# Eleven pairs of heads of the mixer's input projection by Strassen's seven products

## The chip, the cores and the metric

The kernel runs on one core of a Trainium2 chip. The metric is the device time of one execution in microseconds (us). Three timed runs of the kernel before took 2134.25, 2134.5 and 2135.26 us (median 2134.5). The execution whose trace is read here took 2134.78 us; its span, from the first to the last instruction, is 2133.1 us, so 1.7 us lie outside the trace.

## The reference, cut to what matters

A trunk of two layers over 1024 tokens of width 1024, all in float32. Each layer has a token mixer, a norm, a squared-ReLU MLP with a gated embedding beside it, and a norm. The mixer of layer 0 is a pooling, that of layer 1 a gated DeltaNet, whose input projection is the subject here:

```
proj = x @ w_in                                   # 1024x1024 by 1024x4112
qkv, z, b_logit, a_logit = split(proj)            # Q, K, V, z: 8 heads of 128 columns each
qkv = silu(causal_depthwise_conv(qkv, conv_w))    # 4 taps along the tokens
q, k = l2_normalize(q), l2_normalize(k)
beta, g = sigmoid(b_logit), -exp(a_log) * softplus(a_logit + dt_bias)
o = chunk_gated_delta_rule(q, k, v, g, beta)      # 64-token chunks: a triangular solve in each, a scan over them
o = rms_norm(o) * norm_w * silu(z)
mix = o @ w_out
```

The MLP is `square(relu(x @ w1)) @ w2`, with 4096 hidden columns.

## The kernel before, in words

**Products.** Every large product is made in three TensorE matmuls: each operand is cut into a rounded high part and the rest (`split`, L66: a ScalarE copy L68, then a VectorE subtraction L69), and `mm3` (L71, its matmuls L73 to L75) adds high by high, high by rest and rest by high. A full matmul is 128 rows deep, 128 columns of stationary weights wide, and streams 512 columns.

**Order of work.** The stages follow one another: layer 0's mixer, first MLP, DeltaNet, second MLP. `mlp` (L320) already goes by Strassen's scheme. Its first part (L400 ff.) makes the hidden columns in 16 pairs of blocks; a pair is seven products P1 to P7 of twelve matmuls each, 112 products in all, sums of weight blocks are made by VectorE in `prep_a` (L347) three products ahead, and `multiply_a` (L381) runs the products and combines them: P1, P6, P7 and P4 accumulate one after another in one PSUM bank, with a ScalarE copy of the bank between them (L400, L405, L409). Its second part has 56 steps of 24 matmuls, fed by `prep_b` (L451).

**The projection** (`project`, L713) goes over 66 *units*: a unit is one head of K, Q, z or V, or the two gates' columns ("ba"), by half the tokens (512), in 24 matmuls (16 for "ba"), in the order K, Q, z, V (L910 to L914). `load_wsm` (L77) loads a unit's weights and splits them (one 128x1024 split for two units of K, Q and z, for one of V). `conv_a` (L889) convolves a unit of K, Q or V: two ScalarE passes over the PSUM bank and three VectorE passes (L901), then Silu (L902); the results stay in SBUF in six tiles of 16 KB per partition. `z_out` (L904) sends z to DRAM. `at(u, f)` hangs side work on unit u: the decays, the norms of K and Q (`norm2`, transposes on TensorE), `couple` (L822, K by K), then the triangular solve: `lanes_load` fetches a tile L with all 128 blocks, `substitute(m)` eliminates column m in it on VectorE (62 of them, L860 and L862), `lanes_store` and `lanes_turn` send the inverse back to DRAM.

**The scan** (`chain`, L987) goes over 8 chunks of 128 tokens. `load(n)` fetches chunk n's inverse, decays, K transposed and z; `kq`, `kv` and `state_in` read K, Q and V of the chunk from the SBUF tiles through `hc`. `prepare` does chunk 0's part ahead of `run`.

**What sets the order.** The code is straight-line; the framework's list scheduler lays each engine's instructions out once, when the kernel is built, earlier code first among what is ready, and sets the semaphores. On the chip each engine, and SyncE's DMA queue, runs its list in order. Tiles come from pools: `big` has 10 tiles of 16 KB per partition, `wsm` two each of "wh" and "wl", `rawp` three, `tmp` six of 2 KB.

Of the kernel before, what the change touches and what calls it, by code (L numbers as in the profile page):

```python
# [15 lines left out]
P = 128  # L16
S = 1024
# [15 lines left out]
def trunk(ctx: ExitStack, tc: tile.TileContext, io: dict):  # L33
# [286 lines left out]
    def mlp(i, r1, cut_t3, acc, row, finish=None, ahead=None, out=None):  # L320
# [14 lines left out]

        P1, P2, P6, P5, P7, P4, P3 = range(7)
# [3 lines left out]
        with tc.tile_pool(name=f"mlp{i}", bufs=5) as q:  # L340
# [231 lines left out]
    kt_d = dram.tile([8, P, H, P], F32, name="kt_d")  # L572
    ad_d = dram.tile([2, H, 8, 64, 64], F32, name="ad_d")
# [128 lines left out]
    left = mlp(0, r1, cut_t3, acc, 1, finish, ahead)  # L702
# [10 lines left out]
    def project(gd, pool, x2, left, first, heads, g, ex, ahead):  # L713
# [58 lines left out]

        dec = [new_big(F32, "dec").rearrange("p (n c) -> p n c", n=8) for _ in range(2)]
# [90 lines left out]
        def lanes_store():  # L864
# [3 lines left out]
            lanes["Lt"] = new_big(F32, "Lt").rearrange("p (i j) -> p i j", i=64)  # L868

        def lanes_turn(q):  # L870
            L, lt, c = lanes["L"], lanes["Lt"], slice(q * 8, q * 8 + 8)
            A.copy(lt[0:64, c], L[0:64].rearrange("p i j -> p j i")[:, c])
            if q == 7:
                nc.sync.dma_start(t_d.rearrange("h n i j -> (h n) i j"), lt[0:64])
# [9 lines left out]
        def head_tile(s, hf):  # L884
            if (s, hf) not in heads:
                heads[s, hf] = new_big(F32, s).rearrange("p (h c) -> p h c", h=8)
            return heads[s, hf]

        def conv_a(s, h, j, hf, ps):  # L889
            xin = pool.tile([P, 516], F32, tag="xin", name=nm("xin"), bufs=2)  # L890
            y = head_tile(s, hf)[:, h, :]
# [10 lines left out]
            return lambda: A.activation(y, y, AF.Silu)  # L902
# [12 lines left out]
        jof = {"ba": 32, "K": 8, "Q": 0, "z": 24, "V": 16}  # L915
# [14 lines left out]
        K = [head_tile("K", 0), head_tile("K", 1)]  # L930
# [6 lines left out]
        at(20, lanes_load)  # L937

        m, room = 62, 0.0
        for u in range(22, 58):  # L940
            room += 2.2 if u < 34 else 4.2 if u < 50 else 1.5
            while m > 0 and (room > 0 or u == 57):
                at(u, substitute, m)
                room -= 0.4 + 2.1e-3 * m * (63 - m)
                m -= 1
        at(58, lanes_store)
        for q in range(8):
            at(58 + q // 2, lanes_turn, q)
        for k in range(16):
            at(36 + k, lambda k=k: norm2([heads["Q", 0], heads["Q", 1]], g["qn"], k // 2, k % 2))  # L950
        for u, f in ahead:
            at(u, f)
        w = dict(first)

        def weights(k):
            if k < len(units):
                s, h, hf = units[k]
                key = (s, h) if s != "V" else (s, h, hf)
# [5 lines left out]
        for u, (s, h, hf) in enumerate(units):  # L964
# [18 lines left out]
            if fin:  # L983
                fin()
        q_scales()

    def chain(gd, heads, g, ex):  # L987

        hc = lambda s, n, h: heads[s, n // 4][:, h, n % 4 * P:(n % 4 + 1) * P]
# [5 lines left out]
        g4 = lambda gi: slice(gi * 4, gi * 4 + 4)  # L995

        def load(n):
# [12 lines left out]
            nc.sync.dma_start(szt, sz_d[:, :, n * P:(n + 1) * P].rearrange("h d t -> d h t"))  # L1010
# [126 lines left out]
        def prepare():  # L1137
            both(kq, 0)
# [166 lines left out]
```

## Time and profile before

| | busy us | share of the span |
|---|---|---|
| TensorE (PE) | 2106.5 | 99% |
| VectorE (DVE) | 1530.4 | 72% |
| ScalarE (ACT) | 1070.9 | 50% |
| GpSimd (POOL) | 40.3 | 2% |

The profiled execution took 2134.78 us (span 2133.1). The DMA engines moved 308.83 MB at a mean of 145 GB/s; the granted TensorE clock was 0.998 of full speed. "Busy" for TensorE covers overlapping matmuls: one matmul's record is longer than the distance to the next. The shares are means over stages; the first MLP runs from about 172 to 787 us, the projection from 787 to 1190, the scan to about 1302, and the rest of layer 1 to the end.

### The profile page before, as it was taken

To read this page: it belongs to the slowest core of one execution; us is meant where nothing else is said; L and a number is where in the kernel's file an instruction comes from. 1 tells how busy PE (TensorE), PEld (TensorE's weight loads), DVE (VectorE), ACT (ScalarE), POOL (GpSimd) and SP (SyncE) were. 2 spreads that over 40 slices of the span, in tenths; PEclk is the share of its full clock that TensorE was granted. 3 is DMA by queue.
4 is the path that set the end of the run, shared out by engine and by line. 5 is a ranking of instruction groups with operands and counts; after the bars stand their busy time and mean duration, and the time that the engine had idled before them with its cause. 6 is when DMAs were issued, how large, how long until landed. Compare 5 with 4: busy or idle time off the path is not lost.

```text
span 2133.1 us, 27623 instructions
## 1 busy us (share of the span) xinstructions
PE 2106.5 (99%) x10242; PEld 1763.7 (83%) x10242; DVE 1530.4 (72%) x2571; ACT 1070.9 (50%) x1830; POOL 40.3 (2%) x101
## 2 busy tenths in 40 slices
PE   8999999999999999999999999999999999999998
PEld 7888888888888888888888998888888888888887
DVE  7996666668754777879986687499666666875476
ACT  6434555554333457753456676443455555433343
POOL 0000000000000001101001000000000000000000
PEclk9999999999999999999999999999999999999999
DMA  8324444469332333451233655312344445943232
GB/s 307 115 84 148 153 148 144 163 211 335 116 117 99 138 108 104 140 152 50 85 134 114 178 174 178 128 35 86 126 146 163 153 153 185 325 161 119 96 132 88
DMA packets 166154, 308.83 MB, mean 145 GB/s; under 512 B 40258, under 2 KB 62146, under 8 KB 165700
## 3 DMA queue, kind: packets, MB, share of 16 engines
q1 hardware_dynamic: 161412, 298.68, 42.0%
q10 hardware_dynamic: 4608, 8.39, 1.1%
q8 instruction: 80, 1.31, 0.3%
q14 instruction: 54, 0.44, 0.1%
HBM read 212.66 MB, written 94.37 MB: 144 GB/s over the span
## 4 chain that ended last, share of the span: by engine, by line
PE 95%; DVE 2%; ACT 1%; DMA 1%; issue 1%; SPq 0%; DVEq 0%; ACTq 0%
PE ps L73 29%; PE ps L75 29%; PE ps L74 29%; PE ps L143 1%; PE ps L1075 1%; PE ps L1097 1%; PE ps L828 1%; PE ps L799 1%; PE ps L1068 1%; PE ps L1040 1%; PE ps L1063 1%; PE ps L1084 1%; DMA raw<-in_xTt 1%; PE ps L1033 0%; PE ps L1051 0%
## 5 line engine op out<-in xcount | busy, mean ns | idle before, releaser
L74 PE MATMUL ps<-rl,lh 128*128 128x512 f32 x896 | 348.6, 389 | 0.0
L73 PE MATMUL ps<-rh,lh 128*128 128x512 f32 x880 | 342.7, 389 | 0.0
L75 PE MATMUL ps<-rh,ll 128*128 128x512 f32 x880 | 342.3, 389 | 0.0
L68 ACT CAST lh<-raw 128x1024 fp32r<-128x1024 f32 x112 | 118.1, 1055 | 325.5 <-PE ps L74 313.3
L69 DVE TENSOR_TENSOR rl<-w,rh 128x1024 fp32r<-128x1024 f32 x108 | 131.9, 1224 | 178.1 <-issue 107.9
L73 PE MATMUL ps<-xh,wh 128*128 128x512 f32 x512 | 202.7, 396 | 0.0
L75 PE MATMUL ps<-xh,wl 128*128 128x512 f32 x512 | 200.0, 391 | 1.1 <-DVE wl L69 1.1
L73 PE MATMUL ps<-xh,wo 128*128 128x512 f32 x512 | 199.6, 390 | 1.4 <-ACT c L409 1.4
L74 PE MATMUL ps<-xl,wh 128*128 128x512 f32 x512 | 199.4, 390 | 0.0
L75 PE MATMUL ps<-xh,wo 128*128 128x512 f32 x512 | 199.2, 389 | 0.0
L74 PE MATMUL ps<-xl,wo 128*128 128x512 f32 x512 | 199.2, 389 | 0.0
L74 PEld LDWEIGHTS ps<-rl,lh 128*128 128x128 f32 x896 | 168.2, 188 | 34.8
L75 PEld LDWEIGHTS ps<-rh,ll 128*128 128x128 f32 x880 | 165.2, 188 | 34.7 <-DVE ll L69 0.4
L73 PEld LDWEIGHTS ps<-rh,lh 128*128 128x128 f32 x880 | 165.2, 188 | 34.0
L69 DVE TENSOR_TENSOR wo<-raw,wo 128x512 fp32r<-128x512 f32 x192 | 132.1, 688 | 49.9 <-ACT wo L68 49.8
L68 ACT CAST wo<-raw 128x512 fp32r<-128x512 f32 x192 | 119.2, 621 | 96.1 <-PE ps L75 66.1
L339 DVE TENSOR_TENSOR c<-ps,c 128x512 f32<-128x512 f32 x96 | 66.3, 691 | 130.3 <-PE ps L75 67.8
L73 PE MATMUL ps<-xt,wo 128*128 128x512 f32 x384 | 149.6, 390 | 1.5 <-ACT c L400 1.5
L75 PE MATMUL ps<-xt,wo 128*128 128x512 f32 x384 | 149.5, 389 | 0.0
L74 PE MATMUL ps<-xt,wo 128*128 128x512 f32 x384 | 149.4, 389 | 0.0
L69 DVE TENSOR_TENSOR ll<-raw,lh 128x1024 fp32r<-128x1024 f32 x112 | 136.4, 1220 | 1.4 <-ACT lh L68 1.1
L68 ACT CAST rh<-w 128x1024 fp32r<-128x1024 f32 x108 | 112.8, 1047 | 4.4 <-DVE rl L69 2.5
(308 smaller groups left out, 4173.5 us busy)
## 6 DMA issues: line engine op xcount, KB each, us to landing
raw<-h_d SPq DMA_DIRECT2D x112, 512.0 KB, 3.2
raw<-in_w SPq DMA_DIRECT2D x64, 512.0 KB, 3.8
w<-in_w SPq DMA_DIRECT2D x32, 1024.0 KB, 7.6
h_d<-c SPq DMA_DIRECT2D x64, 512.0 KB, 2.8
raw<-in_w_in SPq DMA_DIRECT2D x41, 512.0 KB, 3.5
h_d<-hs SPq DMA_DIRECT2D x32, 512.0 KB, 3.5
pp_d<-tmp ACTq DMA_DIRECT2D x32, 256.0 KB, 3.0
raw<-in_gate SPq DMA_DIRECT2D x16, 512.0 KB, 4.2
```

What stands on the lines that cost most here:

```text
L68: A.copy(hi, src)
L69: V.tensor_tensor(lo, src, hi.bitcast(F32), ALU.subtract)
L73: T.matmul(ps, lh, rh, start=first, stop=False, skip_group_check=more)
L74: T.matmul(ps, lh, rl, start=False, stop=False, skip_group_check=more)
L75: T.matmul(ps, ll, rh, start=False, stop=last, skip_group_check=more)
L143: T.transpose(pss[q][:, j, :], y[:, k * P:(k + 1) * P], ident)
L339: add = lambda o, a, b: V.tensor_tensor(o, a, b, ALU.add)
L799: T.transpose(ps[:, j, :], chunk(tiles, half * 4 + j, h), ident)
L828: T.matmul(ps[:, j, :], kc, kc, start=True, stop=True)
L1040: T.matmul(pq[:, j, :], hc("K", n, h), hc("Q", n, h), start=True, stop=True)
L1063: T.matmul(pk[:, j, :], hc("K", n, h), St[:, h, :], start=True, stop=True)
L1068: T.matmul(pq[:, j, :], hc("Q", n, h), St[:, h, :], start=True, stop=True)
```

## The change

Of the 32 heads of Q, K, V and z, 22 (all of Q and V, six of z) are now projected in 11 pairs. A pair is a 256-column by 1024-token product of depth 1024, made of seven products of 12 matmuls (stationary 128 columns, 512 tokens, depth 512) in place of eight. K, "ba" and two heads of z stay units (22 of them).

The weights' sums, cut into two parts, are made in the first MLP (`pair_parts`: 8 parts for each pair, 88 in all). 60 of them run in the MLP's first part, after products 4 to 107, four to every seven products; 28 in its second part, after steps 8 to 35. They go to DRAM (`ws_d`, 7 tiles of 512 KB a pair) and are fetched again five products ahead of their use. The tokens' sums (`right_a`, `right_b`) are made on the units 9, 11, 18 and 19. `substitute` moves from units 22 to 57 into the pairs (products 3 to 67 of 77), `lanes_store` to product 68, `lanes_turn` to 69 to 72 in eight small tiles, `load0` to 74. K, Q and V go to DRAM (`kqv_d`) and come back by chunk. In a pair the convolution takes all 1024 tokens of a head at once.

```diff
-    def mlp(i, r1, cut_t3, acc, row, finish=None, ahead=None, out=None):
+    def mlp(i, r1, cut_t3, acc, row, finish=None, ahead=None, out=None, side=()):
...
                 multiply_a(*o)
+                if side and 4 <= n < 108 and n * 64 // 112 != (n - 1) * 64 // 112:
+                    side.pop(0)()
...
+                if side and n >= 8:
+                    side.pop(0)()
...
+    pairs = [("Q", 0), ("V", 0), ("z", 2), ("Q", 2), ("V", 2), ("z", 4), ("Q", 4), ("V", 4), ("Q", 6), ("V", 6), ("z", 6)]
...
+    def pair_parts(p):
...
+        def load(key, f, z):
+            t[key] = new_tmp(F32, key)
+            nc.sync.dma_start(t[key], io["w_in"][j + f][:, 4 * z:4 * z + 4, :].rearrange("p k c -> p (k c)"))
+        def cut(k, src=None):
+            hi, lo = new_tmp(F32R, "hi"), t.pop("lo") if src is None else new_tmp(F32R, "lo")
+            src = lo.bitcast(F32) if src is None else src
+            split(hi, lo, src)
+            nc.sync.dma_start(ws_d[p][k][:, 0], hi.bitcast(F32))
+            nc.sync.dma_start(ws_d[p][k][:, 1], lo.bitcast(F32))
+        def s_of(k, o, a):
+            add(t[o], t[o], t[a])
+            cut(k, t[o])
+        return [lambda: (load("a1", 0, 0), load("b1", 1, 0)),
+                lambda: (load("b2", 1, 1), cut(0, t["a1"])),
+                s3,
+                lambda: cut(5, t["b2"]),
+                lambda: (s_of(3, "b1", "b2"), load("a2", 0, 1)),
+                lambda: s_of(2, "a1", "b1"),
+                lambda: cut(1, t["a2"]),
+                lambda: s_of(6, "a2", "a1")]
...
+            def fin():
+                A.activation(y, y, AF.Silu)
+                nc.sync.dma_start(kqv_d[hf * 4:hf * 4 + 4, :, 0, h, :].rearrange("n p c -> p n c"),
+                                  y.rearrange("p (n c) -> p n c", n=4))
...
+            def head(s, h, x, y, n):
+                if s == "z":
+                    A.activation(y, x, AF.Silu)
+                    A.activation(y, y, AF.Copy, scale=nw[:, 0:1])
+                    nc.sync.dma_start(sz_d[h], y)
+                    return
+                A.activation(y, x, AF.Copy, scale=cw[:, j, 3:4])
+                for c in (2, 1, 0):
+                    V.scalar_tensor_tensor(y[:, d:S], x[:, 0:S - d], cw[:, j, c:c + 1], y[:, d:S], ALU.mult, ALU.add)
+                later(n + 1, done, s, h, y, n + 1)
...
+                for kk in range(4):
+                    mm3(ps, o[:, 0, kk, :], o[:, 1, kk, :], right[k][0][:, kk, :], right[k][1][:, kk, :],
+                        new and kk == 0, kk == 3, not new)
+                if k == P1:
+                    A.copy(x11, ps)
+                elif k == P2:
+                    V.tensor_tensor(x11, ps, x11, ALU.add)
+                elif k == P6:
+                    A.copy(x12, ps)
+                elif k == P7:
+                    A.copy(x22, ps)
+                    V.scalar_tensor_tensor(x22, d["ps"][2], -1.0, x22, ALU.mult, ALU.subtract)
+                elif k == P4:
+                    A.activation(x21, ps, AF.Copy, scale=-1.0)
+                    later(n + 1, head, s, h + 1, x[:, 1], x[:, 3], n + 1)
+                elif k == P3:
+                    V.tensor_tensor(x12, ps, x12, ALU.add)
+                    later(n + 1, head, s, h, x[:, 0], x[:, 2], n + 1)
...
-        units += [("Q", h, hf) for h in range(8) for hf in range(2)]
-        units += [("z", h, hf) for h in range(8) for hf in range(2)]
-        units += [("V", h, hf) for hf in range(2) for h in range(8)]
+        units += [("z", h, hf) for h in range(2) for hf in range(2)]
...
+        def right_a(e):
+            mi(r, part(b[1, 1][0], e), part(b[1, 2][0], e))
+            pl(r, r, part(b[1, 1][1], e))
+            mi(r, r, part(b[1, 2][1], e))
+            cut(1, e, r)
+            neg_mi(r2[e], r, b[2, 2], e)
+            cut(2, e, r2[e])
+        def right_b(e):
+            neg_mi(r, r2[e], b[1, 1], e)
+            cut(3, e, r)
+            neg_mi(r2[e], r2[e], b[2, 1], e)
...
+        by_pairs(pool, ts, b)
...
+        def load_kqv(n):
+            if n < 8:
+                t = kqv[n] = new_big(F32, "kqv")[:, 0:3072].rearrange("p (a h c) -> p a h c", a=3, h=8)
+                for a in (slice(0, 2), slice(2, 3)):
+                    nc.sync.dma_start(t[:, a].rearrange("p a h c -> p (a h c)"), kqv_d[n][:, a].rearrange("p a h c -> p (a h c)"))
...
         def prepare():
+            load_sz(pre[0]["szt"], 0)
...
+            load_kqv(1)
...
                 both(state_in, n)
+                load_kqv(n + 2)
```

`load_kqv(0)` is the first thing in `load0`. The order of the seven products, two pairs overlapping, is that of the MLP's first part. Each `neg_mi` is two VectorE passes, each `cut` of the right side one ScalarE and one VectorE pass over 128x1024; after the last unit, two more such cuts follow.

## Rows read from the trace of the kernel before

**Rows 1.** The page's head and its first part: busy us (share) xinstructions.
```profile
span 2133.1 us, 27623 instructions
PE 2106.5 (99%) x10242; PEld 1763.7 (83%) x10242; DVE 1530.4 (72%) x2571; ACT 1070.9 (50%) x1830; POOL 40.3 (2%) x101
```
**Rows 2.** Waits of TensorE: releaser, us in total, times, longest us.
```profile
PE ps L73 <- ACT pT L68: 7.9, 1, 7.9
PE ps L75 <- DVE ol L69: 2.9, 1, 2.9
...
PE ps L73 <- ACT c L409: 1.4, 2, 0.7
```
**Rows 3.** Timeline of TensorE, one V unit: start us, us, instruction.
```profile
1129.83 0.39 PE L73 MATMUL ps<-xh,wh 128*128 128x512 f32 x1
...
1135.27 0.39 PE L73 MATMUL ps<-xh,wh 128*128 128x512 f32 x1
```
**Rows 4.** Groups of instructions: shapes, count | busy us, mean ns | idle before, releasers.
```profile
L73 PE MATMUL ps<-xh,wh 128*128 128x512 f32 x512 | 202.7, 396 | 0.0
...
L69 DVE TENSOR_TENSOR wo<-raw,wo 128x512 fp32r<-128x512 f32 x192 | 132.1, 688 | 49.9 <-ACT wo L68 49.8
...
L68 ACT CAST wo<-raw 128x512 fp32r<-128x512 f32 x192 | 119.2, 621 | 96.1 <-PE ps L75 66.1 <-DVE raw L338 15.4 <-DMA raw<-in_w 8.5
...
L860 DVE TENSOR_TENSOR u<-L 128x468 f32<-128x468 f32 (+45 forms) x123 | 57.9, 507 | 1.5
L862 DVE TENSOR_TENSOR L<-L,u 128x468 f32<-128x468 f32 (+45 forms) x123 | 57.6, 504 | 0.0
...
L901 DVE SCALAR_TENSOR_TENSOR Q<-xin,cw,Q 128x512 f32<-128x512 f32 x48 | 35.7, 745 | 3.8 <-ACT Q L897 3.6
...
L130 DVE SCALAR_TENSOR_TENSOR acc<-acc,lnsm,bc 128x1024 f32<-128x1024 f32 x16 | 20.5, 1280 | 0.3
...
L69 DVE TENSOR_TENSOR xt<-ra,xt 128x1024 fp32r<-128x1024 f32 x8 | 9.7, 1218 | 0.0
```
**Rows 5.** Windows: stretch, us, busy us (xinstructions) of each engine, clock, DMA share, GB/s.
```profile
172.00:478.00 306.00, 304.59 (x1342) 251.38 (x1342) 193.06 (x290) 173.29 (x290) 0.00 (x0) 1.00 0.48 163
478.00:522.00 44.00, 44.00 (x196) 36.45 (x195) 37.15 (x37) 18.43 (x20) 0.00 (x0) 1.00 0.90 321
522.00:675.00 153.00, 153.00 (x677) 126.73 (x676) 96.91 (x94) 56.15 (x56) 0.00 (x0) 1.00 0.38 134
...
787.00:942.00 155.00, 154.10 (x800) 129.81 (x799) 129.14 (x282) 107.13 (x160) 19.96 (x47) 1.00 0.44 131
942.00:1190.00 248.00, 246.89 (x1120) 203.89 (x1119) 203.81 (x374) 122.06 (x289) 16.31 (x44) 1.00 0.35 110
954.00:1100.00 146.00, 146.00 (x671) 120.78 (x670) 143.87 (x293) 61.30 (x179) 6.09 (x16) 1.00 0.24 75
```
**Rows 6.** Timeline of VectorE in a pair of the first MLP.
```profile
304.92 0.69 DVE L339 TENSOR_TENSOR raw<-raw 128x512 f32<-128x512 f32 x1 [1.10 <-DMA raw<-in_w]
...
308.49 0.69 DVE L69 TENSOR_TENSOR wo<-raw,wo 128x512 fp32r<-128x512 f32 x1 [0.22 <-ACT wo L68]
```
**Rows 7.** Timeline of TensorE in the same pair: the first product that uses them.
```profile
312.59 0.39 PE L73 MATMUL ps<-xt,wo 128*128 128x512 f32 x1
```
**Rows 8.** Timeline of VectorE: the last couplings, and the first substitution.
```profile
934.00 4.23 DVE L832 SCALAR_TENSOR_TENSOR at<-ps,ca,dec 128x128 f32<-128x128 f32 x16
...
954.30 0.32 DVE L860 TENSOR_TENSOR u<-L 128x31 f32<-128x31 f32 x2
```
**Rows 9.** DMA issues: KB each, median us from issue to landing.
```profile
L<-ad_d SPq DMA_DIRECT2D x1, 2048.0 KB, 8.1
```
**Rows 10.** Timeline of TensorE: the scan's first matmuls (busy us of the group).
```profile
1189.80 1.95 PE L1040 MATMUL ps<-Q,K 128*128 128x128 f32 x16
```
**Rows 11.** Windows: the stretch with the 2.9 us wait, and the next.
```profile
1320.00:1330.00 10.00, 7.12 (x30) 5.59 (x29) 6.15 (x17) 4.37 (x20) 0.00 (x0) 0.87 0.46 167
1330.00:1340.00 10.00, 10.00 (x44) 8.08 (x44) 2.71 (x8) 4.41 (x11) 0.00 (x0) 0.96 0.07 26
```

More of the change, by code (lines that the diff above doesn't have):

```diff
@@ L701, in trunk @@
              3: [lambda: load_first(("K", 1), None)]}
-    left = mlp(0, r1, cut_t3, acc, 1, finish, ahead)
+    left = mlp(0, r1, cut_t3, acc, 1, finish, ahead, side=parts)
     def sm(pool, s, dt=F32):
@@ L711, in chunk, with project @@
         return tiles[n // 4][:, h, (n % 4) * P:(n % 4 + 1) * P]
-    def project(gd, pool, x2, left, first, heads, g, ex, ahead):
+    def project(gd, pool, x2, left, first, g, ex, ahead, load0):
         xh, xl = x2
@@ L937, in project, with new_r, neg_mi, cut @@
         at(20, lanes_load)
[L939 to L952, printed above, removed]
+        r1, r2, ts = None, {}, {}
+        b = {(r, c): (xh[c - 1][:, 4 * r - 4:4 * r, :], xl[c - 1][:, 4 * r - 4:4 * r, :]) for r in (1, 2) for c in (1, 2)}
+        two = lambda z, e: z[:, 2 * e:2 * e + 2, :]
+        part = lambda z, e: two(z, e).bitcast(F32)
+        pl = lambda o, a, b_: V.tensor_tensor(o, a, b_, ALU.add)
+        mi = lambda o, a, b_: V.tensor_tensor(o, a, b_, ALU.subtract)
+        def new_r(t):
+            return t.rearrange("p (k c) -> p k c", k=2)
+        def neg_mi(o, a, bb, e):
+            V.scalar_tensor_tensor(o, a, -1.0, part(bb[0], e), ALU.mult, ALU.subtract)
+            mi(o, o, part(bb[1], e))
+        def cut(k, e, r):
+            split(two(ts[k][0], e), two(ts[k][1], e), r)
+        def new_t(*ks):
+            for k in ks:
+                t = new_big(F32R, "t").rearrange("p (z k c) -> p z k c", z=2, k=4)
+                ts[k] = t[:, 0], t[:, 1]
+        def right_a(e):
+            r = new_r(pool.tile([P, 1024], F32, tag="u", name=nm("r")))
+            mi(r, part(b[1, 1][0], e), part(b[1, 2][0], e))
+            pl(r, r, part(b[1, 1][1], e))
+            mi(r, r, part(b[1, 2][1], e))
+            cut(1, e, r)
+            r2[e] = new_r(new_raw())
+            neg_mi(r2[e], r, b[2, 2], e)
+            cut(2, e, r2[e])
+        def right_b(e):
+            r = new_r(pool.tile([P, 1024], F32, tag="u", name=nm("r")))
+            neg_mi(r, r2[e], b[1, 1], e)
+            cut(3, e, r)
+            neg_mi(r2[e], r2[e], b[2, 1], e)
+        at(8, new_t, 1, 2)
+        for u, f_, e in ((9, right_a, 0), (11, right_a, 1), (18, right_b, 0), (19, right_b, 1)):
+            at(u, f_, e)
+        at(17, new_t, 3)
+        for u, f_ in ahead:
+            at(u, f_)
         w = dict(first)
@@ L984, in project, with chain @@
                 fin()
+        for e in range(2):
+            split(two(b[1, 2][0], e), two(b[1, 2][1], e), r2[e])
+        ts[4] = b[1, 2]
+        by_pairs(pool, ts, b)
         q_scales()
-    def chain(gd, heads, g, ex):
-        hc = lambda s, n, h: heads[s, n // 4][:, h, n % 4 * P:(n % 4 + 1) * P]
+    def chain(gd, g, ex):
+        kqv = {}
+        hc = lambda s, n, h: kqv[n][:, "KQV".index(s), h, :]
         eg, esuf, etot = ex[:, 0, :], ex[:, 1, :], ex[:, 2, :]
@@ L1200, in run, with load0 @@
             return oT, wk, acc
-        return lambda: load(0), prepare, run
+        def load0():
+            load_kqv(0)
+            load(0)
+        return load0, prepare, run
     def mix_out(oT, wk, acc, stats, t, nh):
@@ L1218, in trunk @@
     with tc.tile_pool(name="gd", bufs=1) as gd:
-        heads, g = {}, {}
+        g = {}
         ex = gd.tile([P, 3, 64], F32, name="ex")
-        load0, prepare, run = chain(gd, heads, g, ex)
+        load0, prepare, run = chain(gd, g, ex)
         with tc.tile_pool(name="gdp", bufs=1) as pool:
-            project(gd, pool, x2, left, first, heads, g, ex, [(64, load0), (65, prepare)])
+            project(gd, pool, x2, left, first, g, ex, [], load0)
+            prepare()
         with tc.tile_pool(name="gdc", bufs=1) as pool:
```

114 lines of the change are left out of this document (99 added, 15 removed).

## The prediction

> **What bounds the kernel now.** I read the page's head first: in a span of 2133.1 us TensorE is busy for 2106.5, so only 26.6 us hold no matmul [rows 1]. The list of TensorE's waits says where these are: 7.9 us at the start, 2.9 us once late, and the next ones are below 1.5 us in all [rows 2]. The windows show the same stage by stage: 304.59 of 306 us in the first MLP's first part, 153.00 of 153 in its second, 154.10 of 155 and 246.89 of 248 in the projection [rows 5]. TensorE's own list of matmuls is the bound in all stages that the change touches. So a matmul taken out there is worth its whole time, and everything that the change adds to VectorE, ScalarE and the DMA costs nothing until it makes TensorE wait.
>
> **The change part by part.**
>
> *Matmuls taken out.* A pair replaces four units of 24 matmuls (96) by seven products of 12 (84); eleven pairs drop 132. The price of one is not its record: records last 396 ns on the mean [rows 4], but overlap. In the timeline 24 matmuls of one unit start from 1129.83 to 1135.27, where the next unit starts: 5.44 us, 0.2267 us each [rows 3]. 132 x 0.2267 = 29.9 us. All 132 stand on the path. The transposes that square Q's norms stay as they are, 64 of them.
>
> By the Trainium skill (TensorE: Matmul & The Clock Gate, part 1), back-to-back matmuls of 512 columns start 215.7 ns apart at the full clock, which would make 28.5 us; and its first page (Trainium Kernel Development and Optimization, Performance Expectations) calls matmul busy time a bad measure because matmuls are pipelined. The trace agrees on the second, and differs on the first by 11 ns, so I stay with the row. Whoever took the 396 ns for the price would expect 52 us.
>
> *Weight sums in the first MLP.* A pair's 8 parts issue 7 splits and 4 additions of 512 columns: VectorE 11 x 0.69 = 7.6 us, ScalarE 7 x 0.62 = 4.3 us [rows 4]; eleven pairs 83 and 48 us. DMAs: 4 loads and 14 stores of 0.262 MB, 4.7 MB. In the first part of the MLP 7.5 pairs fall on 104 products (104 x 12 x 0.2267 = 283 us): VectorE goes from 193.06 of 306 (63%) by 57 us to 83%, ScalarE from 57% to 68%, the DMA from 163 GB/s by 35 MB in 283 us to 288 GB/s, a share of some 0.85. In the second part 3.5 pairs fall on 28 steps (152 us): VectorE from 96.91 of 153 to 81%, DMA from 134 to some 240 GB/s [rows 5]. What hides it: VectorE at 143.87 of 146 us left TensorE at 146.00, and a DMA share of 0.90 at 321 GB/s left it at 44.00 of 44 [rows 5]; the cuts of a product that VectorE starts at 304.92, held 1.1 us by a late load, end at 309.2, and the first product that needs them starts at 312.59, 3.4 us later [rows 6, 7]. SyncE's queue gets 198 more DMAs in order, and a store that waits for its cut holds the weight load behind it by one part's work, some 2 us; that fits into the 3.4. I take 1 us; the ends are 0 and all of VectorE's 83 us.
>
> *Token sums on units 9 to 19.* 24 VectorE passes over 1024 columns at 1.22 us [rows 4]: 29.3 us, ScalarE 6 or 7. VectorE has 129.14 of 155 us busy there [rows 5]; the nine Q convolution passes that fall into this stretch go (9 x 0.745 = 6.7 us), so it comes to 151.7 of 155, 98%, the load that hid well at 143.87 of 146. But unlike the substitutions there, these sums come ahead of the weight cuts of later units in the code, and a cut that is late stops TensorE. I take 1.5 us; the ends are -1 and 22 (29.3 less 6.7 and what is idle).
>
> *The pairs.* Their time on TensorE is 924 x 0.2267 = 209.5 us, and the 7.5 us that 247 less 1056 x 0.2267 leaves for transposes: 217. VectorE has 115.5 us of substitutions, 48 convolution passes of 1.28 (61 us), 33 combinations of 0.69 (23), two cuts and the small ones (6): 206, 95% [rows 4]. It loses 30 weight cuts of 1.22 and 96 passes of 0.745. The copies that free the PSUM bank between P1, P6, P7 and P4 are ScalarE's; in the MLP the same four cost TensorE waits of 0.7 us at most [rows 2]. Convolution, then Silu, then transposes for Q's norms: a late VectorE can hold these. Each product needs 512 KB, with kqv's stores some 250 GB/s, under the 321 above. I take 1 us, ends 0 and 10.
>
> *The way into the scan.* The last couplings end at 938.2 and the first substitution starts at 954.30 [rows 8]; L's load, 8.1 us [rows 9], lies between. The token sums push this by up to 22 us; I take 12, to 966. From there VectorE has the substitutions and seven Q or V pairs (some 188 us by records; I take 177, since records overlap): done at some 1143, then the inverse is turned, stored and loaded, by my estimate to about 1160. The pairs end at 942 + 217 = 1159. The scan now starts with chunk 0's matmuls at 1189.80, the instant that the last unit ends [rows 10]; this margin is gone, and K, Q and V of chunks 0 and 1 (1.5 MB each) have to land too, with z's last store and load ahead of chunk 1 in SyncE's queue. I take 2.5 us; the ends are -1 and 15. Later chunks are loaded a full chunk ahead, 14 us and more: nothing.
>
> *Sum.* -29.9 + 1 + 1.5 + 1 + 2.5 = -23.9. Against the profiled execution: 2134.8 - 23.9 = 2110.9; the median of the runs is 0.3 lower: 2110.6 us.
>
> **The rivals.**
>
> *VectorE holds TensorE in the projection (rival 1).* Place: units 10 to 21, where token sums go ahead of cuts and couplings. For it: 98% busy, nothing left to catch up with, and the delayed substitutions fill the pairs. Against it: the cut for unit 14 could be made from unit 11 on, as the buffer frees then, and TensorE stands still for nobody at 98% in the substitutions. Price: some 10 to 20 of the 22 us, 2134.5 - 29.9 + 15 + 4 = 2124 us.
>
> *The scan waits for its inputs (rival 2).* The inverse or K, Q, V of the first chunks come 10 to 15 us late: 2134.5 - 29.9 + 12 + 3.5 = 2120 us. For it: all stores of the last heads are within 12 us of the end of the pairs. Against it: K and Q of chunk 0 are older, and TensorE has work of chunk 0 to do first. In the one stretch where it stood for 2.9 us the granted clock is 0.87, and 0.96 in the next 10 us, where it was back at work [rows 11]: 1.7 us more lost.
>
> The Trainium skill (TensorE: Matmul & The Clock Gate, part 1) says that idling throttles the array's clock to half and that work releases it; by that rule, and the trace agrees, a stall at the scan's start costs about half as much again.
>
> *The weight parts stand on the path in the first MLP (rival 3, slower).* Each of the 88 parts makes ScalarE copy a sum that VectorE has just made, and ScalarE is in order: the copy that frees the PSUM bank for the next product queues behind it. From 29.9/88 = 0.34 us of TensorE per part the gain is gone. With a part's whole VectorE time (0.95 us) on the path: 2134.5 - 29.9 + 83 = 2188 us. For it: that copy is already a wait of TensorE [rows 2]. Against it: two fifths of VectorE and ScalarE are free there [rows 5] and the cuts are 3.4 us early.
>
> *The pairs are no shorter (rival 4).* If fetching operands from DRAM or the chain of four products in one bank stretches a product from 2.72 to 3.1 us, 77 of them give 29.9 back: 2134 us. Against it: the MLP runs the same scheme with cuts on top at 304.59 of 306.
>
> **How the numbers follow.** Forecast (all four losses together up to 11 us) 0.62; rival 1 0.18; rival 2 0.08; rival 3 0.07 (of this 0.05 slower than before); rival 4 0.05. Range: from -29.9 with nothing lost and 2 us regained (2103) to rival 1's upper end (2126); it leaves out rivals 3 and 4 and little else. About 0.2% (4.3 us) is what a measurement of this kernel tells from no change. Faster by more: 0.62 + 0.18 + 0.08 + 0.02 of the last two = 0.90; within 0.2%: 0.04; slower: 0.06.
>
> **What would show it.** Right: 10110 matmuls in place of 10242; 0.227 us from start to start inside the pairs, 77 products in about 217 us; the first MLP as long as before with VectorE above 80%; waits of TensorE with few new rows, the longest at the scan's start. Rival 1: TensorE waiting for "wh" or "wl" in units 12 to 20. Rival 2: a wait of several us, released by a DMA of kqv, X or t, at the scan's start. Rival 3: a first MLP longer by tens of us. What would make the prediction wrong: many small waits in the first MLP or in the pairs, each below a microsecond, that no single row of before shows.

## The result, and the profile after

The changed kernel is slower: median 2167.8 us (2163.95 to 2171.41, four runs) beside 2134.4 for the kernel before, ratio 1.0157, 95% interval 1.0138 to 1.0175. The forecast was 2110.6 with a range of 2103 to 2126. The profiled execution took 2163.95 us. Its page begins (columns as in [rows 1]):

```profile
span 2162.2 us, 28067 instructions
PE 2091.7 (97%) x10110; PEld 1745.3 (81%) x10110; DVE 1599.7 (74%) x2673; ACT 1089.0 (50%) x1855; POOL 29.3 (1%) x53
```

The 132 matmuls are gone, but the time in which TensorE holds none has grown from 26.6 to 70.5 us (2162.2 less 2091.7). TensorE's waits (columns as in [rows 2]):

```profile
PE ps L1232 <- DMA t<-t_d: 23.0, 3, 19.6
PE ps L73 <- ACT pT L68: 7.9, 1, 7.9
PE ps L73 <- DMA wp<-ws_d: 6.5, 1, 6.5
PE ps L75 <- DVE ol L69: 3.1, 2, 2.9
PE ps L819 <- DVE g L810: 2.8, 1, 2.8
PE ps L75 <- DVE wl L69: 2.6, 1, 2.6
PE ps L73 <- ACT c L411: 2.5, 4, 0.9
```

Two long waits are new: for T, the turned inverse, of the scan's chunk 1, and for a weight of the pairs; g and wl are VectorE's in K's projection. The windows by stage (columns as in [rows 5]; the first stretch is the same as there, the last is the scan's start):

```profile
172.00:478.00 306.00, 302.64 (x1324) 246.95 (x1322) 231.56 (x370) 189.65 (x337) 0.00 (x0) 1.00 0.79 271
...
796.00:958.00 162.00, 153.65 (x787) 128.43 (x786) 147.46 (x297) 113.23 (x164) 23.92 (x40) 0.99 0.50 148
959.00:1191.00 232.00, 221.12 (x996) 180.62 (x995) 190.41 (x341) 95.81 (x224) 1.51 (x3) 0.99 0.78 249
...
1199.00:1223.00 24.00, 7.19 (x41) 7.07 (x42) 1.56 (x2) 4.13 (x10) 0.00 (x0) 0.50 1.03 323
```

Cut at the first product of the first MLP, the first matmul of the gate's columns, the first and the last matmul of the pairs (in the kernel before, of the units that they replace) and the last turn of the scan, both spans fall into stages (us). The two kernels on the right are told of below:

| stage | before | after | forecast change | measured change | no token sums | three causes out |
|---|---|---|---|---|---|---|
| first MLP | 615.3 | 623.4 | +1 | +8.1 | 623.2 | 615.3 |
| gate, K, two z ("K's projection") | 154 | 163.1 | +1.5 | +9.1 | 153.2 | 153.2 |
| pairs | 248 | 232.2 | -29.9 + 1 | -15.8 | 221.9 | 224.5 |
| scan | 171.5 | 199.2 | +2.5 | +27.7 | 200.5 | 176.9 |
| all else | 944.3 | 944.3 | 0 | 0 | 943.9 | 945.4 |
| span | 2133.1 | 2162.2 | -23.9 | +29.1 | 2142.7 | 2115.3 |

So each of the four stages that the change touches came out dearer than forecast. The second MLP, and what else the change doesn't touch, is the same.

### The profile page after: what moved, and what is told of

Its sections match the earlier page's. It is cut to its first block, busy times and chain, and to the rows that moved or that the text cites. A ratio compares the mean times of both kernels' runs of the same rounds, so it can differ in the third digit from the quotient of the medians.

```text
span 2162.2 us, 28067 instructions
## 1 busy us (share of the span) xinstructions
PE 2091.7 (97%) x10110; PEld 1745.3 (81%) x10110; DVE 1599.7 (74%) x2673; ACT 1089.0 (50%) x1855; POOL 29.3 (1%) x53
## 4 chain that ended last, share of the span: by engine, by line
PE 78%; DVE 11%; DMA 5%; ACT 3%; issue 2%; SPq 1%; DVEq 0%; ACTq 0%
PE ps L73 24%; PE ps L75 23%; PE ps L74 23%; DVE u L910 1%; DVE L L912 1%; DVE xy L985 1%; DMA raw<-in_w 1%; PE ps L143 1%; PE ps L1282 1%; DVE ll L69 1%; DVE rl L69 1%; DMA a<-in_w_in 1%; PE ps L1247 1%; PE ps L1304 1%; DMA t<-t_d 1%
## 5 line engine op out<-in xcount | busy, mean ns | idle before, releaser
L69 DVE TENSOR_TENSOR rl<-w,rh 128x1024 fp32r<-128x1024 f32 x108 | 131.9, 1223 | 148.2 <-issue 102.3
L75 PE MATMUL ps<-xh,wo 128*128 128x512 f32 x512 | 199.2, 389 | 0.0
L73 PEld LDWEIGHTS ps<-xh,wo 128*128 128x128 f32 x512 | 96.1, 188 | 24.9 <-ACT c L411 4.5
L75 PEld LDWEIGHTS ps<-xh,wo 128*128 128x128 f32 x512 | 96.1, 188 | 20.0
L74 PEld LDWEIGHTS ps<-xl,wo 128*128 128x128 f32 x512 | 96.1, 188 | 19.7
```

The costliest lines, as they stand in the source:

```text
L69: V.tensor_tensor(lo, src, hi.bitcast(F32), ALU.subtract)
L73: T.matmul(ps, lh, rh, start=first, stop=False, skip_group_check=more)
L74: T.matmul(ps, lh, rl, start=False, stop=False, skip_group_check=more)
L75: T.matmul(ps, ll, rh, start=False, stop=last, skip_group_check=more)
```

## The experiments

Times are medians of four runs; the kernel before ran beside each set (2135.7, 2135.8, 2136.0, 2136.4 and 2136.4 us). Nine profiled runs with the changed kernel's first MLP as it is, its own among them, took 623.2 to 629.0 us for that stage (its own is one of the shortest), so a few us between totals are this stage's scatter, and the stages tell more than the totals.

**1. The order of loads at the scan's start.** SyncE's queue there, and TensorE's timeline (start us, us, what; in brackets idle before and its releaser):

```profile
1191.58 3.13 SPq L979 DMA_DIRECT2D sz_d<-xy  x2
1194.75 0.43 SPq L1198 DMA_DIRECT2D kqv<-kqv_d  x1
1199.95 0.37 SPq L1201 DMA_DIRECT2D first<-sz_d  x1
...
1205.30 3.38 SPq L1213 DMA_DIRECT2D X<-a_d  x1
1208.73 0.72 SPq L1215 DMA_DIRECT2D t<-t_d  x1
```
```profile
1195.04 1.14 PE L1240 MATMUL ps<-first,wt 64*64 64x64 f32 x16
1215.81 1.96 PE L1232 MATMUL ps<-t,X 64*64 64x64 f32 x16 [19.63 <-DMA t<-t_d]
1217.71 3.78 PE L1282 MATMUL ps<-ctr,first 128*128 128x128 f32 x16
```

SyncE issues z's last store, one load, and then nothing until 1199.95: the load of z waits for that store to land, and everything behind it waits too. T of chunk 1 is asked for at 1208.73 and arrives 7 us later. After 19.6 us without a matmul TensorE starts at the lower clock (granted 0.50 from 1199 to 1223, the level of 1.2 GHz): 16 solves in 3.78 us, where 16 matmuls of the same shape took 1.95 us before [rows 10].

```diff
 def prepare():
-    load_sz(pre[0]["szt"], 0)
+    load(1)                 # without its load of z
+    load_kqv(1)
+    for n in range(2): load_sz(pre[n]["szt"], n)
```


> Only the order of SyncE's queue between the last pair and the second chunk of the scan is changed: the inputs of chunk 1 come right behind those of chunk 0, then K, Q and V of chunk 1, then both loads of z; K, Q and V of chunk 2 behind them. Theory (the load of z waits for the last store of z, 5.5 us from its issue, and everything behind it on the queue with it; the wait of 23.0 us for T of chunk 1 is mostly that): the wait falls to under 6 us, the half clock of 1199 to 1223 us goes with it, the time falls by 14 to 22 us, to about 2149. Rival (the transfers are limited by bandwidth, DMA share 1.03 from 1200 to 1220 us): the wait only moves to K, Q and V of chunk 1 or to z, and the time falls by less than 6 us.

Measured 2159.6 us; the scan falls from 199.2 to 191.1, the longest wait for T from 19.6 to 7.0 us. Half of what was expected: both theories hold a part.

**2. The queues too.** In addition to 1:

```diff
-                    nc.sync.dma_start(sz_d[h], y)      # likewise Q's and V's stores
+                    nc.scalar.dma_start(sz_d[h], y)
...
+                both(state_out, n)
+                if n < 7: merge_a(n + 1)               # was ahead of solve(n)
```


> The order of the run with the scan's inputs first (8 us better), and in addition the stores of z, Q and V by the pairs issue from ScalarE's own queue, behind the activation that makes them, and the product with T of chunk n+1 stands behind the state of chunk n instead of ahead of its solve. Theory (SyncE stood from 1192.96 to 1197.29 us at the store of the last z, and T of chunk 1 is asked for by TensorE one step before it is needed): the wait for T falls from 12.8 us to under 3, the half clock goes, 6 to 13 us below the run with the order alone, about 2150. Rival (12 MB of K, Q and V more are loaded in the scan and the transfers are the limit): the wait moves to K, Q, V or X and under 4 us are gained.

2158.7 us; the scan takes 185.2, 14 less than in the changed kernel, and no wait for T is left among the larger ones. In its place stand 4.0 us for K, Q and V and 5.0 at the first solve (the list names no releaser for it, but ScalarE's copy that the solve reads ends 0.1 us before it, and ScalarE had stood for K transposed). The window of this kernel that answers to 1199 to 1223 above:

```profile
1199.00:1222.00 23.00, 15.30 (x105) 14.45 (x106) 7.19 (x20) 11.68 (x27) 0.00 (x0) 0.70 1.07 358
```

The DMA engines are full, and the wait went to K, Q and V, as the rival said, and to K transposed. But the order of the queue has a part in the second of these too. SyncE's list, ScalarE's and TensorE's in this kernel:

```profile
1186.48 0.90 SPq L1215 DMA_DIRECT2D t<-t_d  x1
1194.82 0.33 SPq L1198 DMA_DIRECT2D kqv<-kqv_d  x1
...
1195.67 0.46 SPq L1223 DMA_DIRECT2D ctr<-kt_d  x1
...
1202.90 0.40 ACT L1261 ACTIVATE ctr<-ctr,ex 128x128 f32<-128x128 f32 x1 [2.42 <-DMA ctr<-kt_d]
...
1206.20 3.75 PE L1282 MATMUL ps<-ctr,first 128*128 128x128 f32 x16 [5.03 <-issue]
```

SyncE stands 7.4 us, up to 1194.82, at the load of chunk 0's V until V's last store has landed. Chunk 0's K transposed stands behind that load, though it was sent to DRAM in K's projection, and lands at 1202.88. No run moved it ahead.

**3. Without the reload.** Two kernels, one on the changed kernel and one on that of 2:

```diff
 def load_kqv(n):
+    if n:
+        kqv[n] = kqv[0]
+        return
```


> Leaves out the reload of K, Q and V for chunks 1 to 7: all chunks work on those of chunk 0; the stores stay. The queue orders are those of the changed kernel. Theory A (SyncE's order): T of chunk 1 is still asked for only behind the load of z, the wait stays over 8 us and the scan, 199.2 us from the last product to the last turn, falls by under 12. Theory B (the transfers: DMA share 1.03 at 1200 to 1220 us): the scan falls to within 8 us of the 171.5 of before, 20 us or more down.

> The same left out, on the kernel with the scan's queues changed (2158.7 us, scan 185.7 from last product to last turn). Theory B (what stays there over the 171.5 of before is the 10.5 MB of K, Q and V that come back while everything else of the scan's start is loaded; 358 GB/s from 1200 to 1220 us): the scan falls to 170 to 175 us, 10 to 15 us down. Rival (the order of the work at the scan's start, or its clock): under 5 us down.

2153.3 and 2153.0 us; in the profiled runs the scan takes 186.2 and 180.1. (The medians don't show these 6 us, so the split rests on one profiled run of each kernel.) By it the queues give 14.0 us, the reload left out gives 13.0, and both 19.1 of the 27.7: in part they are one loss. Without the reload its loads are gone from SyncE's queue as well, so the run doesn't part the transfers from the queue. Theory A had said under 12 for the first, theory B 20 or more: neither; and the second lies by the rival's 5. Of the 8.6 that stay, the first solve's 5.6 us and the lower clock after it (0.83 from 1206 to 1226) are the visible part; behind these 5.6 us SyncE stands 7.6 at the load of chunk 0's V, as in 2. What the rest is was not tested.

**4. The token sums.** Five of the seven products take an existing part on their right:

```diff
-right = {P1: b[1, 1], P2: b[2, 1], P6: ts[2], P5: ts[1], P7: ts[3], P4: ts[4], P3: b[2, 2]}
+right = {P1: b[1, 1], P2: b[2, 1], P6: b[2, 1], P5: b[1, 1], P7: b[2, 2], P4: b[1, 2], P3: b[2, 2]}
```


> Leaves out the sums of the token parts: five of the seven products take an existing part on their right. Same matmuls, same weights, same transfers. Theory (VectorE's 16 sums and 16 splits on units 9 to 19 are what lengthened K's projection by 9.3 us and put the couplings' stores late, behind which the third weight of the pairs waits for 6.5 us): from the start of the gate's projection to the first product 154 to 156 us where it was 163.1, the wait for the third weight under 3 us, the time 10 to 16 us down. Rival (K's projection is longer because its first weights and the first MLP's late ends disturb it): under 3 us down.

2145.9 us, 21.9 down, the largest effect of one edit. K's projection falls by 9.9 us and the pairs by 10.3, and the wait for the pairs' weight is gone. Its windows:

```profile
796.00:948.00 152.00, 151.09 (x786) 127.42 (x785) 120.46 (x270) 103.00 (x154) 19.65 (x38) 1.00 0.56 168
949.00:1170.00 221.00, 218.65 (x993) 179.14 (x992) 189.18 (x341) 95.05 (x224) 1.50 (x3) 1.00 0.80 252
```

VectorE goes from 147.46 of 162 us to 120.46 of 152, TensorE from 8.4 us without a matmul to 0.9. The link to the pairs is SyncE's list in the changed kernel:

```profile
946.65 0.66 SPq L972 DMA_DIRECT2D wp<-ws_d  x1
950.11 1.25 SPq L887 DMA_DIRECT2D ad_d<-at  x2
...
957.38 0.67 SPq L888 DMA_DIRECT2D a_d<-at  x1
958.14 2.54 SPq L1074 DMA_DIRECT2D sz_d<-tmp  x2
960.86 0.32 SPq L894 DMA_DIRECT2D L<-ad_d  x1
961.23 3.86 SPq L972 DMA_DIRECT2D wp<-ws_d  x7
```

The second weight goes out at 946.65, the third only at 961.23, behind the stores of the last, late couplings and the load of L; the pairs have begun at 958.8. TensorE waits 6.5 us for it, and from 966 to 975 its granted clock is 0.62.

**5. The sums elsewhere.** On GpSimd (a negation and a subtraction where VectorE had one pass), and late on VectorE:

```diff
-pl = lambda o, a, b_: V.tensor_tensor(o, a, b_, ALU.add)
+pl = lambda o, a, b_: G.tensor_tensor(o, a, b_, ALU.add)     # mi and neg_mi likewise
```


> The sums of the token parts run on GpSimd, their splits stay on ScalarE and VectorE. Theory (VectorE's time in K's projection is what the token sums cost; without them the stage was 9.9 us shorter and the pairs 10.3): both come back in part, 12 to 19 us down. Rival (GpSimd is so slow, or disturbs VectorE so much, that the sums end after the first products): the third product waits longer than 6.5 us, no gain or a loss of up to 15 us.

2196.4 us, 29 up: the rival, and worse. K's projection takes 187 us. Groups of VectorE's instructions there, first in the changed kernel, then in this one (columns as in [rows 4]):

```profile
L945 DVE SCALAR_TENSOR_TENSOR K<-xin,cw,K 128x512 f32<-128x512 f32 x33 | 26.8, 814 | 0.3 <-ACT K L941 0.3
L882 DVE SCALAR_TENSOR_TENSOR at<-ps,ca,dec 128x128 f32<-128x128 f32 x64 | 18.0, 340 | 1.8 <-PE ps L838 1.0 <-POOL dec L842 0.7
L856 DVE TENSOR_REDUCE kn<-tmp 128x4 f32<-128x512 f32 x14 | 9.5, 677 | 0.0
```
```profile
L945 DVE SCALAR_TENSOR_TENSOR K<-xin,cw,K 128x512 f32<-128x512 f32 x33 | 39.7, 1204 | 1.0 <-ACT K L941 0.6
L882 DVE SCALAR_TENSOR_TENSOR at<-ps,ca,dec 128x128 f32<-128x128 f32 x64 | 17.9, 343 | 9.0 <-POOL dec L842 7.6 <-issue 1.1
...
L856 DVE TENSOR_REDUCE kn<-tmp 128x4 f32<-128x512 f32 x13 | 8.8, 680 | 1.4 <-ACT tmp L852 1.4
```

VectorE's passes over two SBUF tiles take half as long again in the mean (814 to 1204 ns), those over PSUM (340, 343) or one tile (677, 680) do not; and the couplings now wait for GpSimd's masks. The mean hides two kinds of passes. One that meets an addition of GpSimd:

```profile
899.16 2.81 POOL L1105 TENSOR_TENSOR raw<-raw,xh 128x1024 f32<-128x1024 f32 x1
899.67 2.85 DVE L945 SCALAR_TENSOR_TENSOR K<-xin,cw,K 128x512 f32<-128x512 f32 x1
```

The seven passes that overlap an addition of GpSimd took 2.3 to 2.9 us, about as long as the addition; of the others in this stage two took 1.41 us and the rest 0.73 to 0.75. This is what the Trainium skill states (SBUF — State Buffer, "SBUF: two separate sides"): VectorE's instructions with two SBUF inputs and GpSimd's that read SBUF exclude each other for a whole instruction. The trace agrees.

```diff
-for u, f_, e in ((9, right_a, 0), (11, right_a, 1), (18, right_b, 0), (19, right_b, 1)):
+for u, f_, e in ((9, right_a, 0), (20, right_a, 1), (20, right_b, 0), (21, right_b, 1)):
...
+start = [(0, P1), (0, P2), (1, P1), (1, P2)]     # then the rest, on slots that the sums don't hold
```


> All work stays. Of the token sums only the first part of four stays inside K's projection, the rest stands behind the last coupling; the pairs begin with four products that need no sum (first and second of pairs 0 and 1), on slots that the sums don't hold. Theory (VectorE is full in K's projection, 142 of 155 us, and each sum there delays TensorE): the stage from gate to first product falls from 163.1 to 156 or less, the third weight's wait shrinks below 3 us, a new wait of up to 8 us for the sums appears in the first pairs; 6 to 15 us down. Rival (the new wait takes it all): within 3 us.

2160.3 us. K's projection falls to 158.3, 4.8 us down where leaving the sums out gave 9.9; the pairs keep their 232.2, with a wait of 4.2 us behind VectorE's substitutions in the place of the weight's, which falls to 1.7. In the pairs the work was moved, not hidden.

**6. The first MLP, half by half.** The weight parts have transfers (44 loads and 154 stores of 0.262 MB, 52 MB; the expectations say 63) and sums and splits. One kernel leaves out the stores, the other the arithmetic:

```diff
-nc.sync.dma_start(ws_d[p][k][:, 0], hi.bitcast(F32))     # and lo: stores left out
```


> The weight parts are made as before but not stored (the 14 stores of 256 KB of each pair are left out; the products read other stored parts of the same size in their place). Theory (the first MLP lost 8.1 us to transfers: 40 MB of stores and 23 MB of loads on a queue at a DMA share of 0.79): the first MLP back to within 2.5 us of before, so 5 to 8 us down. Rival (VectorE's and ScalarE's sums and splits of the parts cost it): within 2 us of the changed kernel.


```diff
-split(hi, lo, src)                                       # and the sums
-nc.sync.dma_start(ws_d[p][k][:, 0], hi.bitcast(F32))
+nc.sync.dma_start(ws_d[p][k][:, 0], src)                 # twice: the loaded tile
```


> The other half: the weight parts' loads and stores stay (the loaded tile is stored twice), their sums and splits are left out. Theory (transfers): within 2.5 us of the changed kernel. Rival (VectorE and ScalarE): the first MLP back to within 2 us of before, 6 to 8 us down. If both this and the run without stores give back a part, the two add.

2155.6 and 2156.9 us; the first MLP takes 615.4 and 615.3 us, the 615.3 of before. Each half alone costs nothing; both cost 8 to 14. Neither theory had that. Two more kernels ask what couples them. First, the same arithmetic on a tile of its own beside the same transfers, for which the small tiles are five instead of six; then arithmetic that reads a constant tile but writes what is stored (both edits in short):

```diff
-split(hi, lo, src)
+split_own()                                # own <- identity, no tie to loads and stores
```


> The weight parts' transfers and as many sums and splits of the same size stay in the first MLP, but the engines work on a tile of their own and never on what is loaded or stored (one slot fewer in the rotating small tiles, to make room): leaves out that the sums are those of the weights. Theory (each half alone costs nothing, since the loss is engines that stand in order at a transfer of the parts while the MLP's own work is behind): both halves of the first MLP at 306.1 and 307.8 us as before, 8 to 12 us down. Rival (the two loads added: VectorE 76% busy and the MLP's own weights landing in 5.4 us instead of 3.7): the MLP's first half stays 3 us or more over 306.1.


```diff
-A.copy(hi, src); V.tensor_tensor(lo, src, hi, subtract); stores of hi and lo
+A.copy(hi, ident); V.tensor_tensor(lo, ident, hi, subtract); stores of hi and lo
```


> The weight parts' loads, sums, splits and stores all stay, in the same number and on the same small slots, but the sums and splits read a tile that is always there and never the loaded ones (leaves out that they are sums of the weights). So engines and stores wait for each other as in the changed kernel, and no engine waits for a load of the parts. Theory A (the first MLP's loss comes from the side of the stores: slots that come free only when a store has landed, SyncE standing at a store): its halves stay 3 us or more over 306.1 and 307.8. Theory B (it comes from engines that stand in order at a load of the parts): both halves at 306.1 and 307.8.

2162.6 and 2158.8 us. The first part's window, in the first of them and in the second:

```profile
172.00:478.00 306.00, 304.74 (x1341) 251.12 (x1340) 245.25 (x386) 200.08 (x347) 0.00 (x0) 1.00 0.81 280
```
```profile
172.00:478.00 306.00, 304.60 (x1342) 251.45 (x1342) 235.23 (x370) 195.21 (x341) 0.00 (x0) 1.00 0.80 275
```

Both have more of VectorE's time, and as much DMA, as the changed kernel's 231.56 and 0.79, and TensorE starts its full 1341 or 1342 matmuls there ([rows 5]: 1342; changed kernel: 1324). So the load on the engines is not the price. The first MLP took 615.5 and 616.7 us. (In the first, the free arithmetic ran in the first part altogether, so it says nothing of the second part; in the second kernel the second part is 1.5 us longer than before.) What is missing in both is an engine that waits for a load of the parts. The second kernel misses one thing more: nobody reads the loaded tiles, so their slots come free early, and the waits of ScalarE and VectorE for a store to free a slot, some 19 us in the changed kernel's first MLP, are gone as well. So it leaves loads or slots as the cause; 7 tells more. In the changed kernel VectorE waits 7.8 us for such loads in the first part, and ScalarE 17.1 in the second (172 to 478 us, with the wait for the MLP's own weights, and 478 to 785):

```profile
DVE raw L341 <- DMA raw<-in_w: 43.7, 15, 3.9
DVE lo L590 <- DMA b<-in_w_in: 7.8, 7, 2.0
```
```profile
ACT hi L68 <- DMA a<-in_w_in: 17.1, 5, 5.3
```

The longest of TensorE's new waits in this MLP can be followed back to such a load:

```profile
578.72 0.62 ACT L68 CAST hi<-a 128x512 fp32r<-128x512 f32 x1 [5.28 <-DMA a<-in_w_in]
579.38 0.69 DVE L69 TENSOR_TENSOR lo<-a,hi 128x512 fp32r<-128x512 f32 x1 [1.62 <-ACT hi L68]
...
582.86 1.22 DVE L69 TENSOR_TENSOR rl<-w,rh 128x1024 fp32r<-128x1024 f32 x1
584.13 0.50 PE L74 MATMUL ps<-rl,lh 128*128 128x512 f32 x1 [1.44 <-DVE rl L69]
```

ScalarE stands at the load, VectorE then 1.62 us for ScalarE's half; from there VectorE works without a pause, and `rl`, which the MLP's product needs, comes 1.44 us late.

**7. Remedies for the first MLP.** SyncE stands 81.9 us of the first stretch at stores of `hi`:

```profile
SPq L600 <- ACT hi L68: 81.9, 36, 5.8
SPq L601 <- DVE lo L69: 17.2, 21, 1.7
```

So the stores went to two other queues, and then the loads were issued earlier:

```diff
-nc.sync.dma_start(ws_d[p][k][:, 0], hi.bitcast(F32))
+nc.gpsimd.dma_start(ws_d[p][k][:, 0], hi.bitcast(F32))   # lo likewise; the second kernel: hi by nc.scalar
```


> All work of the change stays; only the stores of the weight parts are issued from GpSimd's queue, which is idle in the first MLP, instead of SyncE's. Theory (SyncE's queue is in order, and each of these stores waits for ScalarE's or VectorE's half, 81.9 us for hi alone from 172 to 478 us; the MLP's own weight loads stand behind them, and VectorE waits 43.7 us for those where it waited 12.6): VectorE's wait for the raw weights falls below 20 us, the first MLP to within 3 us of before, 6 to 11 us down. Rival (the 63 MB themselves, DMA share 0.79, make every transfer late): the wait stays near 40 us and the time within 3 us.

> All work stays; the store of each part's high half is issued by ScalarE, which has just made it, instead of by SyncE, which stood 81.9 us at these stores from 172 to 478 us with the MLP's own loads behind. Theory (SyncE's stand is what makes the raw weights late): VectorE's wait for them falls from 43.7 to under 25 us and the first MLP's halves lose 2 us each or more. Rival (the slots and the parts' loads hold VectorE and ScalarE, whoever issues the stores): the first MLP within 2 us of the 8 to 13 us over before that its runs show.

2206.6 and 2180.1 us, 39 and 12 up; the first MLP took 663.8 and 634.2. VectorE's wait for the raw weights didn't fall (51.5 and 46.5 us). Either queue brings a loss of its own; of GpSimd's only this much is seen, that VectorE then waits 18.4 us for stores to free their slots. In the second kernel SyncE's stand only moved, to the stores of `lo` (75.7 us in that stretch), so these two don't settle whether it is the cause; the next two do.

```diff
-lambda: (load("a1", 0, 0), load("b1", 1, 0)),      # first step of its pair
+# now at the end of step 7 of the pair before; b2 and a2 one step sooner
```


> All work stays; each load of the weight parts is issued one or two steps of the parts earlier (the first two parts of a pair in the second last step of the pair before, the third and fourth one step sooner), on the same six small slots. Theory (the first MLP loses time because VectorE and ScalarE stand in order at these loads; with engines that never wait for them its first half took 306.0 us and its second 309.3): the halves fall by 2 us each or more from the 310 to 314 and 312 to 314 of the runs so far, 4 to 9 us down in all. Rival (the slots are the limit: an earlier load only waits, on SyncE's queue, for a slot to come free, with the MLP's own loads behind): no gain, or a loss of up to 10 us.

> All work of the change, with the scan's queues changed and the loads of the weight parts earlier. If both help by themselves, 2150 to 2154; if the slots are the limit, 2155 to 2170. Either way above the kernel before, since the token sums (some 20 us) and the rest of the scan's start stay.

2163.2 and 2153.3 us; the first MLP took 620.2 and 616.8, beside the 623.2 to 629.0. Earlier loads bring back a good half of the loss. In the whole first MLP the waits of ScalarE and VectorE for loads of the parts fall from 31.3 us in the changed kernel to 1.3 and 0.7. What else could be the cause stays: VectorE's wait for the raw weights is 41.3 and 37.4 us in the first stretch, and SyncE's stand at the stores is as long as in the changed kernel (99.4 us in all in the first of the two, beside 99.1):

```profile
SPq L600 <- ACT hi L68: 70.2, 45, 5.7
SPq L601 <- DVE lo L69: 29.2, 43, 1.7
```

So the waits for loads cost a good half of it, and SyncE's stand at the stores by itself little. At the earlier loads SyncE stands 6.4 us in all for a free slot, in the changed kernel not at all. The engines' waits for a store to free a slot fall less, from 19.1 us to 17.5 and 11.4; whether the 4.9 and 1.5 us that are left are theirs was not tested. That the two kernels differ by 3.4 us in a stage with the same code was not followed up.

**8. Together.** The GpSimd variants with the scan's queues, the two helpful edits that keep all work, and all causes left out:

> The three edits together. Theory (three separate losses of about 9, 18 and 20 us): they add, the time is 2120 to 2132, below the kernel before. Rival (they share one cause, the transfers): less than the sum by 10 us or more, still over 2134.

> All work of the change, with the two edits that helped and change no arithmetic: the scan's queues and the late token sums. Theory (separate losses): they add, 2160.3 less some 8 us, 2150 to 2154. Rival (the same transfers at the end of the pairs are behind both): above 2156.

> All three causes out at once: the weight parts' sums and splits, the token sums, and the reload of K, Q and V for chunks 1 to 7 are left out, the scan's queues are changed; the products, their 132 matmuls fewer, all stores and all other loads stay. Theory (these are the whole of what went wrong, and the pairs give the predicted 29.9 us): first MLP 614, gate to first product 153, pairs 222, scan 180, in all 2115 to 2121, below the kernel before by 14 to 20. Rival (something else of the change costs time that these hid): over 2128.

2232.0, 2162.0 and 2117.6 us. The first is the sum of its parts and a little more (39 + 29 - 9 = 59 up, measured 64). The second is no better than either edit: its first MLP took 627.9, and its pairs 236.8, so late sums and new queues don't add. The best whole version is that of 7 with the scan's queues, 2153.3, still 0.81% (0.65 to 0.98) above before. The third is the closing test: without arithmetic on parts, token sums and reload, and with the scan's queues of 2, the products save their time, ratio 0.9911 (0.9895 to 0.9926), within the 2115 to 2121 that were expected. Its windows from the first MLP on:

```profile
173.00:788.00 615.00, 613.59 (x2720) 507.26 (x2720) 400.67 (x533) 300.16 (x432) 0.00 (x0) 1.00 0.70 241
789.00:941.00 152.00, 151.10 (x787) 127.41 (x786) 120.58 (x271) 103.02 (x154) 20.27 (x40) 1.00 0.57 168
942.00:1166.00 224.00, 220.60 (x996) 180.86 (x995) 189.21 (x341) 95.45 (x224) 1.56 (x3) 0.99 0.79 252
```

Every stage but the scan (5.4 us over before, 2.5 forecast), and some 5 us of the pairs, is where the forecast had it or better.

## Why the prediction was wrong, step by step

*Matmuls taken out (-29.9): right.* 10110 matmuls, 0.227 us from start to start. Undisturbed pairs take 221.9 us; 248 - 29.9 = 218.1, and the 0.9 us of 8 of chunk 0's 16 matmuls of K and Q, which moved into them, make 219.0.

*Weight sums (+1): 8.1, with scatter up to 14.* The busy shares were forecast too high if anything (VectorE 83%, measured 231.56 of 306; DMA 0.85, measured 0.79), and the conclusion still failed. TensorE lost the time in five waits of 0.2 to 1.4 us and in some 27 delays of under 0.25 us, close to the many small waits that the prediction names last as what would make it wrong. The step that failed is "a store that waits for its cut holds the weight load behind it by one part's work, some 2 us; that fits into the 3.4". The margin of 3.4 us was read from a pair in which nobody waited for a part. I had priced a late store and not a late load: VectorE and ScalarE, in order, stand at a load of the parts (31.3 us in all) with the MLP's cuts behind them; with the loads earlier 1.3 and 0.7 us of these waits are left, and 4.9 and 1.5 us of the loss. Rival 3 named the place and the order of ScalarE's list; its price per part was ten times too high (8.1/88 = 0.09 us in place of 0.95).

*Token sums (+1.5): 9.1 here and 10.3 in the pairs.* Rival 1's mechanism, in its place; the wait for wl that was to show it is in the list (2.6 us), with g and the decay's operands beside it. I argued that TensorE stood still for nobody while VectorE was at 98%; but those were substitutions with nobody behind them, while here K's cuts, couplings and gates stand behind the sums. And I followed the pushed couplings only to L, not to the weights of the pairs that are queued behind their stores on SyncE.

*The pairs (+1): 13 over the 219.1 of the forecast.* The token sums' 10.3 and the moved 0.9 are named; with the 1 us of the forecast 2.9 stay for what the pairs themselves cost, well inside the bounds of 0 and 10. Rival 4 fell: the spacing of matmuls inside products is unchanged.

*The way into the scan (+2.5, at most 15): 27.7.* This is the largest miss, outside both bounds. The margin was indeed gone, and rival 2 named the wait and its releaser. But I priced lateness of single inputs and not two things. The prediction names z's last store and load as ahead of chunk 1 in SyncE's queue and asks no price for it: z's load stands at z's last store with all later loads behind it (the queues gave 14.0 us back). And at that moment K, Q and V, which before never left SBUF, join the inverse, decays, K transposed and z in the same 30 us, at a DMA share of 1.03 (13.0 us came back without the reload, 19.1 with both edits; 8.6 stay open). And "later chunks [...]: nothing" was wrong by some 4 us: from chunk 1's first solve to the last turn the changed kernel takes 154.5 us, and 150.1 without the reload (149.9 before).

*The chances.* I gave 0.90 to faster, treating the rivals as alternatives, of which one comes at most. Three of the rivals came at once; each of them stands in VectorE's list or in SyncE's queue.

## What to carry to other kernels

A window in which TensorE stays full at a high share of VectorE or DMA shows only that *that* work hid; ask of new work who stands behind it in each in-order list, and above all whether an engine with urgent work will stand at a DMA. When data that stayed in SBUF is sent through DRAM, add up every transfer of the 30 us around the hand-over, and look in the DMA queue for a load that waits for a store: all loads behind it wait as well. Price losses that share an engine or a queue as one case, and take all of them out together in one run to see whether the list of causes is complete.

## What the runs showed of the hardware that was not expected

- 52 us more of VectorE's time than before (245.25 beside 193.06) at a DMA share of 0.81 cost TensorE nothing in the first MLP's first part, and less arithmetic with as much DMA cost 4 to 8 us, once the arithmetic had to wait for the transfers.
- GpSimd's additions over two SBUF tiles took 2.4 to 3.4 us each for 128x1024, and the seven of VectorE's two-tile passes of 128x512 that overlapped one took 2.3 to 2.9 us in place of 0.75.
- With the DMA engines full (share 1.03 to 1.07, 323 to 358 GB/s), loads of 128 KB (in pieces of 256 bytes) took 7 to 10 us to land, as long as those of 1 MB (7.6 to 8.2).
